# A two-layer diffusion trunk on one Trainium2 core: normed loads put first in the sync queue, and one context product moved into the group before

## The chip, the cores and the metric

The kernel runs on one core of one Trainium2 chip. Its time is the device time of one execution in microseconds (us), given as the median of several runs; lower is better.

## The reference

Two layers work on 1024 latent tokens and 256 context tokens of width 1024. Layer 0 mixes the tokens by attention and a linear recurrence side by side, layer 1 by neighbourhood attention; each layer then has a feed-forward part (ConvFFN). The change lies where layer 0 goes from its mixer to its ConvFFN, in these lines:

```python
y_lat = jnp.concatenate([oa_lat, readout(ob_lat, bg_l)], axis=-1) @ w_out
x = x + g1 * rms_norm(y_lat, norm_post_mix[l])
h_lat = rms_norm(x, norm_pre_ffn[l]) * (1.0 + sc2) + sh2
x = x + g2 * rms_norm(conv_ffn(h_lat, ...), norm_post_ffn[l])
# the same for the context tokens, with their own modulation

def conv_ffn(h, w_up, conv_w, conv_b, w_down):
    u = h @ w_up                                   # 1024 -> 5632
    u = depthwise_width_3_conv(u) + conv_b         # over the positions
    a, g = jnp.split(u, 2, axis=-1)
    return (jax.nn.silu(g) * a) @ w_down
```

## The kernel before

**Arithmetic.** Every fp32 operand of a product is split into a high and a low part (names that end in h and l), and each product is three matmuls: high by high, high by low, low by high. All matmuls come from one helper, so nearly all have line L120; they are told apart by tile names.

**The end of the mixer** (`even_attention`). Five blocks of 256 tokens (the context first, then four of latent tokens) go through attention; `project` is a generator that multiplies finished blocks by the output weights (tiles `g_ps`) in small steps, given out between the attention's own steps by `step(n)`. Each output tile of 128 tokens has closing work, kept in the list `late` and taken from it one piece at a step: root mean square, gate, residual, the store of the new stream to `x1d`, a second root mean square, a scaling on ScalarE (L1038), and the store of the normed tile to the DRAM tensor `xnd` (L1039). There are ten such tiles: 8 and 9 are the context, 0 to 7 the latent tokens. Tile 7 is closed last. `step` does nothing while the next block is not ready.

**The start of the ConvFFN** (`ffn_up`, and in it `up_front`, for layer 0). The ten tiles are loaded back from `xnd` as `n_x` (L1413), 512 KB each. TensorE transposes them (L1147) into three PSUM banks in turn (`n_pv`, `n_pc`, `n_pt`); ScalarE applies scale and shift (L1148); VectorE and ScalarE split the results. First come the context tiles (8, 9), then the first half of the latent tokens (tiles 0 to 3), then the second half (4 to 7), then sums of these.

**The up projection** is done by 22 groups. A group takes 128 columns of each of the two halves of `w_up`, two loads of 512 KB named `w_raw` (L1333), and forms the latent product by a scheme of seven block products in place of eight: A11·B11, A12·B21, S2·T2, S1·T1, S3·T3, A22·T4 and S4·B22, where A and S are weights and their sums, and B and T are activations and their sums. They go into the banks `u_g` and `u_v`. The context product has two halves of 24 matmuls of 256 columns each, one with A11 and A12 and one with A21 and A22, into the bank `u_pc`. In group 0 the sums T1, T3, T4 and the split of B22 are still being made, between the products that read them.

**What sets the order.** Inside `in_order(engines)` the instructions of those engines keep the order in which the code is written. `even_attention` does this for all engines and the sync queue (SyncE, SP in the profile); `ffn_up` for the four computing engines only, so that its DMAs on the sync queue are ordered by a scheduler. A DMA waits in its queue for its semaphores, and those behind it in the queue wait with it. Memory is handed from a closed pool to the next when the last reader of the overlapped tiles is done. The loop over the groups, at the start of a group:

```python
                if ctx and j:
                    pc = pp.tile([P, 512], F32, name="u_pc", bufs=1)
                    product(pc[:, :256], ("A11", "A12"), "ctx", True, True)
                elif ctx:
                    pc = st["pc"]
```

Here `j` is the group, and `st["pc"]` is the tile that `up_front` filled for group 0.

Of the kernel before, what the change touches and what calls it, by code (L numbers as in the profile page):

```python
# [11 lines left out]
F32 = mybir.dt.float32  # L12
# [8 lines left out]
P = 128  # L21
D = 1024
# [43 lines left out]
class Trunk:  # L66
# [785 lines left out]
    def even_attention(self, gp, tp, pp, sp):  # L852
# [5 lines left out]
        nc, a = self.nc, self.a  # L858
# [3 lines left out]
        st = {}  # L862
# [8 lines left out]
        def load_gate(kind):  # L871
            g = st["gate"] = sp.tile([P, D], F32, name="gate", bufs=1)
            nc.sync.dma_start(g, self.gated[0, 0, kind].partition_broadcast(P))
# [117 lines left out]
        def gated(b, k):  # L991

            step(32 * b - at[0])
            split(b, BH + k, st["g", b][:, k, :])
            if k == BH - 1:
                st["ready"] = b

        def squares(y, ms):
            junk = sp.tile([P, 512], BF16, name="yjunk", bufs=1)
            for h in range(2):  # L1000
                nc.scalar.activation(junk, y[:, 512 * h:512 * h + 512], AF.Square, scale=1.0 / 32.0, accum_out=ms[:, h:h + 1])

        def project():

            late = []
            for b, (n0, kind) in enumerate(blocks):
                for i in range(2):
                    y = sp.tile([P, D], F32, name="y", bufs=2)
                    ms = self.small.tile([P, 2], F32, name="y_ms")
                    for half in range(2):  # L1010
                        ps = gp.tile([P, 512], F32, name="g_ps")
                        for k in range(KT):
                            xhk, xlk = (o[:, i * P:(i + 1) * P] for o in st["o", b, k])
                            whk, wlk = (w[:, 512 * (k % 2):512 * (k % 2) + 512] for w in W[4 * half + k // 2])
                            self.mm(ps, xhk, whk, k == 0, False)
                            self.mm(ps, xhk, wlk, False, False)
                            self.mm(ps, xlk, whk, False, k == KT - 1)
                            if late:
                                late.pop(0)()
                            yield b  # L1020
                        late.append(lambda ps=ps, y=y, ms=ms, half=half: self.y_half(ps, y, ms, half, sp))
                        if half == 0:
                            xt = sp.tile([P, D], F32, name="y_x", bufs=2)
                            r = n0 + i * P
                            nc.sync.dma_start(xt, a["ctx"][i * P:(i + 1) * P] if kind else a["x"][r:r + P])
                        else:
                            late.append(lambda ms=ms: st.update(r=self.y_rstd(ms)))
                            late.append(lambda: None)
                            late.append(lambda: None)
                            late.append(lambda y=y: self.y_norm(y, st["r"], st["gate"]))  # L1030
                            late.append(lambda y=y, xt=xt: nc.vector.tensor_tensor(out=y, in0=y, in1=xt, op=OP.add))
                            late.append(lambda: None)
                            late.append(lambda y=y, r=r: nc.gpsimd.dma_start(self.x1d[r:r + P], y))
                            ms2 = self.small.tile([P, 2], F32, name="y_ms")
                            late.append(lambda y=y, ms2=ms2: squares(y, ms2))
                            late.append(lambda ms2=ms2: st.update(r2=self.y_rstd(ms2)))
                            late.append(lambda: None)
                            late.append(lambda y=y, xt=xt: nc.scalar.mul(xt, y, st["r2"]))  # L1038
                            late.append(lambda xt=xt, r=r: nc.gpsimd.dma_start(self.xnd[r:r + P], xt))  # L1039
                    if b == 0 and i == 1:  # L1040
                        late.append(lambda: load_gate(0))
            while late:
                late.pop(0)()

        fill, todo, at = project(), [], [0]

        def step(n):

            for _ in range(n):
                if at[0] < 32 * (st.get("ready", -1) + 1):  # L1050
                    next(fill, None)
                    at[0] += 1

        zeros = sp.tile([P, 2 * LINE], F32, name="zeros", bufs=1)[:, 0:1]
        nc.gpsimd.memset(zeros, 0.0)
# [2 lines left out]
        with self.in_order(*self.compute, E.SP):  # L1058
# [9 lines left out]
            for s in range(N + 8):  # L1068
# [11 lines left out]
                t = transposes(pair - 2, half) if 0 <= pair - 2 < len(pairs) else iter(())  # L1080
# [243 lines left out]
    def ffn_up(self, l, src, ctx, x_src, x_dst, hp, pp, tp, es, beside):  # L1324


        nc, a = self.nc, self.a
        raws, W, S, st = {}, {}, {}, {}

        def load(j, s):  # L1330
            if j < FK:
                raws[j, s] = self.wp.tile([P, 1024], F32, name="w_raw", bufs=3)
                nc.sync.dma_start(raws[j, s], a["w_up"][l, j + FK * s])  # L1333
# [19 lines left out]
        def product(ps, ws, x, start, stop):  # L1353

            jobs = [(W[w], k) for w in ws for k in range(4)]
            for i, ((wh, wl), k) in enumerate(jobs):
                h, lo = wh[:, k * P:(k + 1) * P], wl[:, k * P:(k + 1) * P]
                xhk, xlk = X[x][i]
                self.mm(ps, h, xhk, start and i == 0, False)
                self.mm(ps, h, xlk, False, False)  # L1360
                self.mm(ps, lo, xhk, False, stop and i == len(jobs) - 1)

        def add(out, x, y):
            nc.vector.tensor_tensor(out=out, in0=x, in1=y, op=OP.add)  # L1364
# [36 lines left out]
        def up_front():  # L1401
# [3 lines left out]
            xs, turn = {}, [0]  # L1405
            tags = dict(zip((8, 9, 0, 1, 2, 3, 4, 5, 6, 7), ["x_T" + x for x in ("20h", "20l", "21h", "21l", "30h", "30l")] +
                            ["x_T1" + x for x in ("0h", "0l", "1h", "1l")]))
            for i, t in tags.items():
                if i == 4:
                    load(0, 0)  # L1410
                    load(0, 1)
                xs[i] = hp.tile([P, D], F32, name="n_x", tag=t, bufs=1)
                nc.sync.dma_start(xs[i], self.xnd[i * P:(i + 1) * P])  # L1413

            def places():
                turn[0] += 1
# [103 lines left out]
        with self.in_order(*self.compute, behind=l == 1), ExitStack() as loads:  # L1520
# [3 lines left out]
            for j in range(FK):  # L1524
                n = j + 1
                if n == FK:
                    loads.enter_context(self.in_order(mybir.EngineType.SP))
                    down = self.ffn_down(l, ctx, x_src, x_dst, hp, sp, pp, tp, beside)
                    next(down)
                if ctx and j:  # L1530
                    pc = pp.tile([P, 512], F32, name="u_pc", bufs=1)
                    product(pc[:, :256], ("A11", "A12"), "ctx", True, True)
                elif ctx:
                    pc = st["pc"]
# [26 lines left out]
                        split(n, "A12")  # L1561
                Z = st["G", j][:, 512:]
                product(Z, ("S1",), "T1", True, False)
                u2 = st["u2"] = half("f_u2")
                add(u2, V[:, 512:], st["p1"])
                if j == 0:
# [1061 lines left out]
```

## Time and profile before

| | us |
|---|---|
| median of 3 runs | 3382.82 |
| the three runs | 3382.82, 3382.61, 3395.19 |
| the profiled execution | 3393.66 |
| its span, first to last instruction | 3391.9 |
| TensorE busy in it | 3124.3 (92%) |
| last matmul of layer 0's mixer starts at | 1109.08 |
| first transpose of layer 0's ConvFFN starts at | 1123.67 |
| group 1 of the up projection starts at | 1195.20 |

Times inside the execution count from the start of the span. PE is TensorE, PEld its weight loads, DVE VectorE, ACT ScalarE, POOL GpSimd, and SPq the DMA issues of the sync queue. A row of the timeline holds start, duration, engine, line, operation, out<-in with shapes, and in brackets how long the engine had been idle before it and what ended that.

### The profile page before, as it was taken

The numbers are of one execution on the slowest core, as the hardware profiler recorded it, in microseconds if no ns is written. First come the engines' busy times: TensorE is split into PE (matmuls) and PEld (weight loads), VectorE is DVE, ScalarE is ACT, GpSimd is POOL, SyncE is SP. The second block draws the span as 40 slices with busy tenths as digits, with TensorE's granted clock in tenths as the row PEclk, the third lists the DMA queues.
The fourth block names the chain that finished last, engine by engine and source line by source line (L and its number), as shares of the span: only waits on it lengthen the run. The fifth ranks groups of instructions, "written<-read, shape, count | busy, mean of one in ns | idle before, by whom it ended". The sixth has DMA issues, their size and how long they took to land.

```text
span 3391.9 us, 48795 instructions
## 1 busy us (share of the span) xinstructions
PE 3124.3 (92%) x18364; PEld 2569.4 (76%) x18364; DVE 2020.3 (60%) x3405; ACT 1501.8 (44%) x2681; POOL 1545.7 (46%) x1173
## 2 busy tenths in 40 slices
PE   5999998869999699999999979999998989999997
PEld 2777776658887488888878758889886758888785
DVE  3635666647776654454567873367775465555777
ACT  3322222256665543343434353366665543434443
POOL 1310110187775466666620011477775367777201
PEclk8999999979999799999999989999998979999998
DMA  6534333321111321111275783222224212222855
GB/s 235 156 98 138 119 130 108 114 89 44 63 57 68 121 73 69 65 70 69 74 258 180 276 247 128 79 60 71 63 59 158 102 62 81 87 81 81 279 183 208
DMA packets 202540, 398.73 MB, mean 118 GB/s; under 512 B 23344, under 2 KB 84784, under 8 KB 202304
## 3 DMA queue, kind: packets, MB, share of 16 engines
q1 hardware_dynamic: 191680, 358.38, 31.7%
q0 software_dynamic: 10624, 37.23, 2.9%
q8 instruction: 144, 2.36, 0.3%
q14 instruction: 92, 0.75, 0.1%
HBM read 316.86 MB, written 79.06 MB: 117 GB/s over the span
## 4 chain that ended last, share of the span: by engine, by line
PE 75%; DVE 10%; ACT 4%; DMA 4%; issue 3%; POOL 2%; SPq 1%; ACTq 0%; POOLq 0%; DVEq 0%
PE g_ps L120 21%; PE u_g L120 13%; PE u_v L120 10%; PE d_ps L120 10%; PE u_pc L120 4%; PE a_pv L120 2%; PE c_pv L120 2%; PE c_s L120 2%; PE a_pt L950 2%; PE c_pt L2258 2%; PE mod_ps L120 1%; DVE a_pl L952 1%; PE a_s L120 1%; PE o_ps L120 1%; ACT a_ph L951 1%
## 5 line engine op out<-in xcount | busy, mean ns | idle before, releaser
L128 POOL TENSOR_TENSOR rs_r<-rs_e,mhalf 128x1 f32<-128x1 f32 (+3 forms) x106 | 80.7, 761 | 953.0 <-DVE rs_e L127 952.9
L120 PE MATMUL d_ps<-d_Bh,d_Ah 128*128 128x512 f32 x704 | 278.0, 395 | 12.0 <-ACT d_Bh L1672 11.9
L120 PE MATMUL d_ps<-d_Bl,d_Ah 128*128 128x512 f32 x704 | 278.4, 396 | 3.4 <-DVE d_Bl L1673 2.7
L120 PE MATMUL d_ps<-d_Bh,d_Al 128*128 128x512 f32 x704 | 277.3, 394 | 2.0 <-DVE d_Al L1673 1.9
L2241 POOL TENSOR_SCALAR c_p<-c_p,rl 128x640 f32<-128x640 f32 (+1 forms) x128 | 232.2, 1815 | 96.3 <-DVE rl L2240 58.9
L930 POOL TENSOR_SCALAR a_p<-a_p,rl 128x1280 f32<-128x1280 f32 (+1 forms) x80 | 240.2, 3007 | 56.8 <-DVE rl L929 52.5
L120 PE MATMUL g_ps<-xh,w_hi 128*128 128x512 f32 (+1 forms) x640 | 259.6, 406 | 6.3 <-ACT w_hi L564 4.9
L120 PE MATMUL g_ps<-xh,w_lo 128*128 128x512 f32 (+1 forms) x640 | 240.3, 376 | 2.5 <-POOL w_lo L2141 1.3
L120 PE MATMUL g_ps<-xl,w_hi 128*128 128x512 f32 (+1 forms) x640 | 240.8, 376 | 0.0
L952 DVE TENSOR_TENSOR a_pl<-a_pt,a_ph 128x512 fp32r<-128x512 f32 (+1 forms) x200 | 119.0, 603 | 92.3 <-ACT a_ph L951 92.3
L1364 DVE TENSOR_TENSOR f_u<-u_v,f_p 128x512 f32<-128x512 f32 x88 | 60.5, 688 | 188.5 <-PE u_v L120 188.5
L120 PEld LDWEIGHTS d_ps<-d_Bh,d_Ah 128*128 128x128 f32 x704 | 133.9, 190 | 42.0 <-ACT d_Bh L1672 13.5
L1350 POOL TENSOR_TENSOR w_S4l<-w_s,w_S4h 128x512 fp32r<-128x512 f32 x44 | 57.0, 1297 | 233.8 <-ACT w_S4h L1349 233.8
L120 PEld LDWEIGHTS d_ps<-d_Bl,d_Ah 128*128 128x128 f32 x704 | 133.9, 190 | 36.2 <-DVE d_Bl L1673 7.7
L120 PEld LDWEIGHTS g_ps<-xh,w_hi 128*128 128x128 f32 x640 | 123.9, 194 | 45.8 <-issue 27.7
L120 PEld LDWEIGHTS d_ps<-d_Bh,d_Al 128*128 128x128 f32 x704 | 133.8, 190 | 30.9 <-DVE d_Al L1673 3.3
L951 ACT CAST a_ph<-a_pt 128x512 fp32r<-128x512 f32 (+1 forms) x200 | 101.9, 518 | 108.7 <-PE a_pt L950 108.6
L2261 DVE TENSOR_TENSOR c_pl<-c_pt,c_ph 128x256 fp32r<-128x256 f32 (+1 forms) x256 | 113.1, 470 | 58.5 <-ACT c_ph L2260 57.3
L120 PE MATMUL g_ps<-w_hi,xh 128*128 128x512 f32 (+1 forms) x368 | 142.7, 388 | 3.1 <-DVE xh L2015 2.1
L120 PEld LDWEIGHTS g_ps<-xh,w_lo 128*128 128x128 f32 x640 | 123.4, 193 | 25.8 <-POOL w_lo L2141 1.7
L120 PE MATMUL g_ps<-w_lo,xh 128*128 128x512 f32 (+1 forms) x368 | 138.5, 376 | 3.7 <-DVE w_lo L2002 2.9
L120 PE MATMUL g_ps<-w_hi,xl 128*128 128x512 f32 (+1 forms) x368 | 138.6, 377 | 0.2 <-DVE xl L300 0.2
(543 smaller groups left out, 9873.5 us busy)
## 6 DMA issues: line engine op xcount, KB each, us to landing
m_raw<-in_w_mod SPq DMA_DIRECT2D x96, 512.0 KB
w_raw<-in_w_up SPq DMA_DIRECT2D x88, 512.0 KB
d_rawA<-actd SPq DMA_DIRECT2D x77, 512.0 KB
d_rawB<-in_w_down SPq DMA_DIRECT2D x74, 512.0 KB
actd<-f_t SPq DMA_DIRECT2D x22, 640.0 KB
d_t<-in_w_down SPq DMA_DIRECT2D x22, 512.0 KB
actd<-f_t SPq DMA_DIRECT2D x22, 512.0 KB
d_s<-actd SPq DMA_DIRECT2D x20, 512.0 KB
```

Source lines behind the costliest of these rows:

```text
L120: return self.nc.tensor.matmul(out, lhsT, rhs, start=start, stop=stop, skip_group_check=True, **k)
L128: nc.gpsimd.tensor_tensor(out=r[:p, :n], in0=e[:p, :n], in1=self.mhalf[:p, :n], op=OP.pow)
L930: nc.gpsimd.tensor_scalar(Pt[:, :nk], Pt[:, :nk], rl, None, op0=OP.mult)
L950: nc.tensor.transpose(pt[:, m, qt * P:(qt + 1) * P], Pt[:, kts[j + m] * P:(kts[j + m] + 1) * P], self.ident)
L951: nc.scalar.copy(ph[:, j:j + n], pt[:, :n])
L952: nc.vector.tensor_tensor(out=pl[:, j:j + n], in0=pt[:, :n], in1=ph[:, j:j + n].bitcast(F32), op=OP.subtract)
L1350: nc.gpsimd.tensor_tensor(out=lo, in0=part(j, name), in1=hi.bitcast(F32), op=OP.subtract)
L1364: nc.vector.tensor_tensor(out=out, in0=x, in1=y, op=OP.add)
L2241: nc.gpsimd.tensor_scalar(Pt[:, :n], Pt[:, :n], rl, None, op0=OP.mult)
L2258: nc.tensor.transpose(pt[:, j, :], Pt[:, (src + j) * P:(src + j + 1) * P], self.ident)
L2261: nc.vector.tensor_tensor(out=vap(pl, o, dims), in0=pt[:, :cnt], in1=vap(ph, o, dims).bitcast(F32), op=OP.subtract)
```

## The change

Three edits, all in layer 0.

1. The list `late` is made outside `project`, and `step` takes a piece from it when the next block is not ready. In the built program the order on ScalarE, VectorE and GpSimd is row by row what it was: at no step that finds its block not ready does the list hold anything.
2. The loop that loads the ten `n_x` tiles keeps its written order on the sync queue.
3. The first half of group 1's context product (24 matmuls) is written in group 0, behind S1·T1 and ahead of S3·T3, into the transposes' bank `n_pt`. Groups 2 to 21 are as they were.

```diff
+        late = []
+
         def project():
-            late = []
             for b, (n0, kind) in enumerate(blocks):
...
                 if at[0] < 32 * (st.get("ready", -1) + 1):
                     next(fill, None)
                     at[0] += 1
+                elif late:
+                    late.pop(0)()
...
-            for i, t in tags.items():
-                if i == 4:
-                    load(0, 0)
-                    load(0, 1)
-                xs[i] = hp.tile([P, D], F32, name="n_x", tag=t, bufs=1)
-                nc.sync.dma_start(xs[i], self.xnd[i * P:(i + 1) * P])
+            with self.in_order(mybir.EngineType.SP):
+                for i, t in tags.items():
+                    if i == 4:
+                        load(0, 0)
+                        load(0, 1)
+                    xs[i] = hp.tile([P, D], F32, name="n_x", tag=t, bufs=1)
+                    nc.sync.dma_start(xs[i], self.xnd[i * P:(i + 1) * P])
...
-                if ctx and j:
+                if ctx and j > 1:
                     pc = pp.tile([P, 512], F32, name="u_pc", bufs=1)
                     product(pc[:, :256], ("A11", "A12"), "ctx", True, True)
                 elif ctx:
                     pc = st["pc"]
...
                 Z = st["G", j][:, 512:]
                 product(Z, ("S1",), "T1", True, False)
+                if ctx and j == 0:
+                    st["pc"] = tp.tile([P, 512], F32, name="u_pc", tag="n_pt", bufs=1)
+                    product(st["pc"][:, :256], ("A11", "A12"), "ctx", True, True)
```

The sync queue, between the last load of the mixer and the third weight load. The numbers tell the tiles apart: `n_x_11128` and `11130` are tiles 8 and 9, `11132` to `11138` tiles 0 to 3, `11144` to `11150` tiles 4 to 7; `w_raw_11140` and `11142` are the weights of group 0, `11233` the first of group 1. Before:

```order
L1025 DMA y_x_11035<-in_x 128x1024
L1333 DMA w_raw_11140<-in_w_up 128x1024
L1333 DMA w_raw_11142<-in_w_up 128x1024
L1413 DMA n_x_11144<-xnd_80 128x1024
L1413 DMA n_x_11146<-xnd_80 128x1024
L1413 DMA n_x_11148<-xnd_80 128x1024
L1333 DMA w_raw_11233<-in_w_up 128x1024
L1413 DMA n_x_11128<-xnd_80 128x1024
L1413 DMA n_x_11130<-xnd_80 128x1024
L1413 DMA n_x_11132<-xnd_80 128x1024
```

The same place in the change:

```order
L1026 DMA y_x_11035<-in_x 128x1024
L1417 DMA n_x_11128<-xnd_80 128x1024
L1417 DMA n_x_11130<-xnd_80 128x1024
L1417 DMA n_x_11132<-xnd_80 128x1024
L1417 DMA n_x_11134<-xnd_80 128x1024
L1417 DMA n_x_11136<-xnd_80 128x1024
L1417 DMA n_x_11138<-xnd_80 128x1024
L1336 DMA w_raw_11140<-in_w_up 128x1024
L1336 DMA w_raw_11142<-in_w_up 128x1024
L1417 DMA n_x_11144<-xnd_80 128x1024
L1417 DMA n_x_11146<-xnd_80 128x1024
```

The context tiles and tiles 0 to 3 have moved ahead of the weights and of tiles 4 to 6; the third weight load now comes behind tile 7 and behind the load of the convolution's taps (`cw`).

TensorE in group 0, between S1·T1 (`x_T11` with `w_S1`) and S3·T3 (`x_T30` with `w_S3`). Before:

```order
L120 MATMUL u_g<-x_T11h,w_S1h 128x512
L120 MATMUL u_g<-x_T11l,w_S1h 128x512
L120 MATMUL u_g<-x_T11h,w_S1l 128x512
L120 MATMUL u_v<-x_T30h,w_S3h 128x512
L120 MATMUL u_v<-x_T30l,w_S3h 128x512
L120 MATMUL u_v<-x_T30h,w_S3l 128x512
```

In the change, the last rows of the product that has come between:

```order
L120 MATMUL u_pc<-x_ctx3h,w_A12h 128x256
L120 MATMUL u_pc<-x_ctx3l,w_A12h 128x256
L120 MATMUL u_pc<-x_ctx3h,w_A12l 128x256
L120 MATMUL u_v<-x_T30h,w_S3h 128x512
L120 MATMUL u_v<-x_T30l,w_S3h 128x512
L120 MATMUL u_v<-x_T30h,w_S3l 128x512
```

The 24 matmuls of `u_pc` stand in front of S3·T3. TensorE from group 0 to group 1, between S4·B22 (`x_B221` with `w_S4`) and what follows, before:

```order
L120 MATMUL u_g<-x_B221h,w_S4h 128x512
L120 MATMUL u_g<-x_B221l,w_S4h 128x512
L120 MATMUL u_g<-x_B221h,w_S4l 128x512
L120 MATMUL u_pc<-x_ctx0h,w_A11h 128x256
L120 MATMUL u_pc<-x_ctx0l,w_A11h 128x256
```

And in the change:

```order
L120 MATMUL u_g<-x_B221h,w_S4h 128x512
L120 MATMUL u_g<-x_B221l,w_S4h 128x512
L120 MATMUL u_g<-x_B221h,w_S4l 128x512
L120 MATMUL u_g<-x_B210h,w_A12h 128x512
L120 MATMUL u_g<-x_B210l,w_A12h 128x512
```

Group 1 now opens with A12·B21 (`x_B210` with `w_A12`); the context product is gone from there.

## The prediction

> **What bounds the kernel now.** I read the page first (engines, chain), then the PE's waits, then a table by stage around the change, then the timeline of each engine there.
>
> ```profile
> PE 3124.3 (92%) x18364; PEld 2569.4 (76%) x18364; DVE 2020.3 (60%) x3405; ACT 1501.8 (44%) x2681; POOL 1545.7 (46%) x1173
> PE n_pv L1147 <- DMA n_x<-xnd: 15.7, 2, 14.2
> 1109.50:1123.70 14.20, 0.03 (x1) 0.06 (x1) 3.73 (x7) 3.28 (x7) 2.24 (x4) 0.62 0.96 354
> 1123.70:1155.50 31.80, 25.99 (x140) 19.86 (x140) 22.55 (x36) 22.44 (x38) 12.37 (x9) 0.85 0.25 102
> 1165.90:1195.20 29.30, 17.34 (x36) 10.05 (x37) 20.22 (x28) 12.79 (x22) 14.10 (x11) 0.65 0.17 54
> 1195.20:1740.00 544.80, 542.06 (x2858) 467.58 (x2856) 276.74 (x308) 215.00 (x299) 343.87 (x247) 1.00 0.24 85
> ```
>
> A stage row is length, then busy time of PE, PEld, DVE, ACT and POOL, clock, DMA share, GB/s. TensorE bounds the whole, and from 1195.2 the up projection runs on it without a gap (542.06 of 544.80): what arrives there earlier ends earlier. Ahead of that it stands still twice: 14.2 us for `n_x`, the longest wait of its kind in the trace, with the DMA engines full (0.96), and some 12 us in group 0 (29.30 less 17.34), where VectorE has the larger share.
>
> **The closing pieces** (edit 1) move nothing, since the built order on ScalarE, VectorE and POOL is the old one: 0.
>
> **The loads** (edit 2). The sync queue before:
>
> ```profile
> 1099.94 0.33 SPq L1025 DMA_DIRECT2D y_x<-in_x  x1
> 1109.50 1.00 SPq L1333 DMA_DIRECT2D w_raw<-in_w_up  x2
> 1110.55 1.39 SPq L1413 DMA_DIRECT2D n_x<-xnd  x3
> 1111.98 0.47 SPq L1333 DMA_DIRECT2D w_raw<-in_w_up  x1
> 1112.55 13.85 SPq L1413 DMA_DIRECT2D n_x<-xnd  x7
> 1134.07 0.33 SPq L1464 DMA_DIRECT2D cw<-in_convT  x1
> 1082.41 1.19 PE a_pv L120 x10
> ```
>
> After the last `y_x` the queue stands until the last matmul of the mixer frees the weights' memory (1109.5); then two weights, tiles 4 to 6 and one more weight go ahead of the context tiles that TensorE needs first. In the change, tiles 8, 9 and 0 to 3 stand behind `y_x`, and what they wait for on the way (scores and values of the attention's last heads; the last row, from the chain of waits) is over by 1083.6. They issue from 1100.3, six at about 0.4 us each. The slowest rate seen here: eight loads from 1109.50 until tile 9 lets its transpose start at 1125.65 are 4.2 MB in 16.2 us, 260 GB/s. At that rate `y_x` and the context tiles (1.57 MB) are in by 1106.4, and all seven (3.7 MB) by 1114.4.
>
> The end of the wait is then no longer a load:
>
> ```profile
> 1117.21 1.15 ACT L1038 ACTIVATE y_x<-y,rs_r 128x1024 f32<-128x1024 f32 x1 [1.12 <-POOL rs_r L128]
> 1126.16 0.56 ACT L1148 ACTIVATE n_t<-n_pv,mod,mod 128x256 f32<-128x256 f32 x1 [7.80 <-PE n_pv L1147]
> 1147.44 0.62 ACT L1349 CAST w_A11h<-w_raw 128x512 fp32r<-128x512 f32 x1 [0.34 <-issue]
> 1125.65 0.47 PE L1147 MATMUL n_pv<-ident,n_x 128*128 128x128 f32 x1 [1.53 <-DMA n_x<-xnd]
> 1139.50 0.60 PE L1147 MATMUL n_pc<-ident,n_x 128*128 128x128 f32 x4
> 1118.65 0.57 POOL L1039 DMA_DIRECT2D xnd<-y_x  x1 [1.48 <-ACT y_x L1038]
> xnd<-y_x POOLq DMA_DIRECT2D x4, 512.0 KB, 3.0
> ```
>
> TensorE can fill its three transpose banks at about 1111, but ScalarE, whose order is kept, first closes tile 7; its scaling ends at 1118.36. So of the 14.2 us only ScalarE's own gap goes, **7.8 us**. From 1126.16 to group 0 the work is a chain of ScalarE and VectorE with TensorE between, none of it tied to the clock on the wall, and it moves by 7.8 as a whole, if the other loads keep up.
>
> Each queue neighbour has room. Tile 7 is read back after its store, issued at 1118.65. Before, that store had full DMA engines beside it and the last `n_x` issued only at 1126.4 (end of the row of seven). Even then, with the 3.0 us from issue to landing that the last row has for 512 KB, tile 7 is there at 1129.4, and is wanted at 1139.50 − 7.8 = 1131.7. Behind it wait `cw` and the first weight of group 1, which by the same 3.0 us lands at about 1130 and is wanted at 1147.44 − 7.8 = 1139.6. Group 0's weights issue at 1109.5 as before. So 0 for these; if tile 7 were later than 1131.7 each us would cost one.
>
> **The context product** (edit 3). The new place, TensorE and then VectorE:
>
> ```profile
> 1165.47 0.40 PE L120 MATMUL u_g<-x_T11h,w_S1l 128*128 128x512 f32 x1
> 1167.48 0.49 PE L120 MATMUL u_v<-x_T30h,w_S3h 128*128 128x512 f32 x1 [1.61 <-ACT x_T30h L1133]
> 1168.82 0.50 PE L120 MATMUL u_v<-x_T30l,w_S3h 128*128 128x512 f32 x1 [0.85 <-DVE x_T30l L1136]
> 1171.15 0.79 PE L120 MATMUL u_v<-x_T30h,w_S3h 128*128 128x512 f32 x1 [1.60 <-ACT x_T30h L1133]
> 1167.45 1.31 DVE L1136 TENSOR_TENSOR x_T30l<-x_t,x_T30h 128x512 fp32r<-128x512 f32 x1 [0.68 <-ACT x_T30h L1133]
> ```
>
> The chain of waits gives the prices of the products:
>
> ```profile
> 1144.44 0.74 PE u_g L120 x2
> 1146.05 2.88 PE u_pc L120 x24
> 1149.80 2.75 PE u_g L120 x12
> 1183.91 4.73 PE u_v L120 x11
> 1190.99 4.37 PE u_g L120 x11
> ```
>
> The product takes 2.88 us. Put in at 1165.70 it ends at 1168.58, and the second matmul of S3·T3 could not start before 1168.76 anyway; 1.6 us more of slack follow. So it costs nothing where it goes and takes 2.88 us from the full stretch after 1195.2. Part of this comes back in group 1, where the rest isn't faster:
>
> ```profile
> 1210.42 0.56 ACT L1367 ACTIVATE f_t<-u_pc,cw 128x256 f32<-128x256 f32 x1 [0.66 <-DMA actd<-f_t]
> 1213.17 0.48 DVE L1372 SCALAR_TENSOR_TENSOR f_t<-u_pc,cw,f_t 128x255 f32<-128x255 f32 x1
> 1214.80 0.69 DVE L1364 TENSOR_TENSOR f_u<-u_v,f_p 128x512 f32<-128x512 f32 x1 [1.15 <-PE u_v L120]
> 1215.53 0.70 DVE L1364 TENSOR_TENSOR u_v<-u_g,f_u 128x512 f32<-128x512 f32 x1
> 1214.61 0.39 PE L120 MATMUL u_g<-x_B110h,w_A11h 128*128 128x512 f32 x1
> ```
>
> The convolution of group 1's context waits for the store of group 0's result (0.66 us on the DMA), which hangs on group 0's VectorE work, not on the product. VectorE is free at 1213.65 in both kernels; it then makes `f_u` and the sum that reads `u_g` (0.73 and 0.70 us), 1215.08, and S4·B22 may not write `u_g` before that. TensorE, which starts the twelve matmuls ahead of it at 1214.61 (last row) and ends them 2.75 later (the chain's row for twelve), would be there at 1217.36 − 2.88 = 1214.48. So 0.6 us are lost, and **2.3 us** stay. At worst the gain is 0 (VectorE as late as 1217.4), at best 2.88; I take 2.3, being read from the rows.
>
> **The clock.**
>
> ```profile
> 1112.00:1116.00 4.00, 0.00 (x0) 0.00 (x0) 2.49 (x2) 1.35 (x4) 0.56 (x1) 0.62 1.01 373
> 1132.00:1136.00 4.00, 3.33 (x21) 2.83 (x20) 3.90 (x7) 3.94 (x7) 1.51 (x2) 0.82 0.08 23
> 1168.00:1172.00 4.00, 1.53 (x3) 0.58 (x3) 3.32 (x3) 0.62 (x1) 3.50 (x3) 0.88 0.27 108
> 1184.00:1188.00 4.00, 4.00 (x10) 3.13 (x11) 1.67 (x3) 3.03 (x6) 2.97 (x2) 0.50 0.01 2
> 1182.76 0.80 PE L120 MATMUL u_v<-x_T40h,w_A22h 128*128 128x512 f32 x1 [5.39 <-ACT x_T40h L1133]
> ```
>
> The granted clock (third number from a row's end) falls to half after the long wait (0.62 in the row of 1112: 0.96 us full and 3.04 half, so at about 1113.0), is back by the same reckoning at about 1133.4, and falls again at about 1171.0, so that A22·T4 and most of S4·B22 ran at half (4.73 and 4.37 us for eleven). The Trainium skill (TensorE: Matmul & The Clock Gate, "What's actually happening") says that the clock is judged by free-running windows of 3.413 us, halved after an idle one and restored after a busy one; the trace agrees, the three edges lying 20.4 and 37.6 us apart, 6 and 11 such windows. In the change TensorE still idles from about 1112 to 1118 and still 5.4 us before A22·T4, so I add 0, with ±2 us for where the edges fall.
>
> **The sum.** 7.8 + 2.3 = 10.1 us. The profiled execution took 3393.66 (span 3391.9), so it would take 3383.6. It lies 10.8 above the median of 3382.82, close to the slowest run shown (3395.19); I carry the difference over: **3372.7 us**. That is 0.3%, less than the 0.5% (16.9 us) that a measurement of this kernel can tell from no change.
>
> **The rivals.**
> *The clock stays full.* The moved product keeps TensorE busy through a gap, the fall at 1171.0 is avoided, and A22·T4 and S4·B22 run at full rate. Eleven matmuls at 2.75/12 are 2.5 us: 2.2 + 1.9 = 4.1 more, 3368.6. Against it: the 5.39 us of idle, which the product doesn't touch. Chance 0.10. By the window rule just named the fall merely comes later.
> *The loads alone.* The 2.3 us come back too, in group 1 or behind it: 3375.0, chance 0.09.
> *A new wait for the same stage.* The 3.1 MB issued at 1100.3 hold up what closes tile 7 or brings it back, and ScalarE starts the context no sooner: 3380.5. It decides if `y_x` lands later than 1113.3, or tile 7 later than 1139.5. Against it, `y_x` is ahead in the same queue. Chance 0.06.
> *Slower: half clock through the front.* TensorE now works in short bursts from 1111, is judged idle longer, and the five products of twelve and two of 24 up to 1165.9 all run at half: 5 × 2.75 + 2 × 2.88 = 19.5 more, 3392.2, and more if it lasts into group 1. It decides if the clock isn't back by 1136.6 (1144.4 − 7.8, where products begin to set the time). Against it, the transposes brought it back at 1133.4. Chance 0.05.
> *The level of the run.* The runs shown lie 12.6 us apart, and one trace doesn't say why: with the forecast's gain the upper level gives 3385.3 (0.09), and if the cause of the upper level lies in this wait too, the other way, 3360.1 (0.11).
>
> **The numbers.** The forecast has the remaining 0.50, with 3369 to 3377 as its own range. From 3365 to 3386 lie the forecast, the first three rivals and the upper level, 0.84 less their tails, so 8 in 10. Faster by over 0.5% (below 3365.9): 0.11 and 0.03 from the clock rival's best end, 0.14. Slower by over 0.5% (above 3399.7): 0.03, from the slow rival where it lasts. Within: 0.83.
>
> **What would show it.** The first `n_x` issues at about 1100.3, the wait for `n_x` is gone from the PE's list, and the first `n_t` follows directly on the last L1038, 7.8 us earlier. `u_pc` of group 1 lies before S3·T3 with no later start of the second matmul there; group 1's S4·B22 shows a wait of some 0.6 us for VectorE; the start of group 2 is 10 us earlier. I am wrong if a wait for `n_x` is left, if tile 7 is waited for, or if the clock is half between 1137 and 1158.

## The result, and the profile after

| | before | changed |
|---|---|---|
| median of 7 runs each, us | 3385.20 | 3373.03 |
| lowest and highest | 3382.61, 3395.19 | 3368.97, 3377.46 |
| changed to before, with 95% interval | | 0.9956 [0.9940, 0.9971] |
| profiled execution; its span | 3393.66; 3391.9 | 3373.03; 3371.3 |

The changed kernel is 12.2 us (0.36%) faster in the medians. Its time lies within the forecast's own range, its gain below the 0.5% (16.9 us) named there, and the interval of the ratio does not hold 1. First, the waits of the PE in the changed kernel (engine, line waited for, us in total, times, longest). Line numbers are 1 to 4 higher than before.

```profile
PE n_pv L1150 <- ACT n_t L1151: 7.0, 1, 7.0
```

The row for `n_x`, 14.2 us in one piece before, is gone from the whole list. In its place TensorE, its three banks filled, waits 7.0 us for ScalarE to empty the first. The reason is in the timelines of the sync queue and of ScalarE, changed kernel:

```profile
1096.49 0.33 SPq L1026 DMA_DIRECT2D y_x<-in_x  x1
1096.91 2.88 SPq L1417 DMA_DIRECT2D n_x<-xnd  x6
1106.05 0.96 SPq L1336 DMA_DIRECT2D w_raw<-in_w_up  x2
1107.06 13.26 SPq L1417 DMA_DIRECT2D n_x<-xnd  x4
...
1113.77 1.15 ACT L1039 ACTIVATE y_x<-y,rs_r 128x1024 f32<-128x1024 f32 x1 [1.12 <-POOL rs_r L128]
1114.82 0.55 ACT L1151 ACTIVATE n_t<-n_pv,mod,mod 128x256 f32<-128x256 f32 x1
```

Six `n_x` issue 0.42 us after `y_x`, where the first `n_x` stood 10.6 us behind it before, and the first `n_t` follows tile 7's scaling without a gap (before, 7.80 us lay between). The table by stage (length, then busy time of PE, PEld, DVE, ACT and POOL, granted clock, DMA share, GB/s) has the end of the mixer in its first row, then group 0 up to S1·T1, the rest of group 0, and the groups up to layer 0's down projection:

```profile
1105.63:1115.42 9.79, 1.26 (x8) 0.64 (x7) 3.76 (x8) 3.79 (x9) 1.88 (x4) 0.70 1.02 413
1115.42:1155.94 40.52, 35.44 (x182) 28.03 (x183) 32.17 (x46) 26.98 (x45) 19.66 (x14) 0.86 0.23 81
1155.94:1185.22 29.28, 18.71 (x61) 12.12 (x60) 20.47 (x28) 12.79 (x22) 14.37 (x11) 0.71 0.17 54
1185.22:1740.00 554.78, 551.75 (x2889) 475.07 (x2889) 287.45 (x319) 220.84 (x306) 344.09 (x247) 1.00 0.26 92
```

The DMA engines are still full in the first row (1.02), but no engine waits for them there. The third row holds the moved product: 61 matmuls, where the stretch before had 36 in a nearly equal 29.30 us.

By the starts that the timelines show, the two profiles and the spread over all thirteen profiles of this case (us):

| stretch | before | changed | all thirteen |
|---|---|---|---|
| start to the first matmul of attention's scores | 726.5 | 723.0 | 719.4 to 728.6 |
| on to the mixer's last matmul | 382.6 | 382.6 | 379.4 to 384.1 |
| on to the first `n_t` (**first stage**) | 17.08 | 9.19 | by kernel |
| on to group 2 (**second stage**) | 93.89 | 92.41 | by kernel |
| on to the first matmul of the down projection | 495.9 | 495.9 | 495.9 to 496.0 |
| on to the end | 1675.9 | 1668.1 | 1668.1 to 1677.9 |

Of the 20.6 us between the two spans only 7.9 + 1.5 lie where the code changed. The rest lies in stretches whose code is the same, and which differ by up to 10 us between any two profiles. So the two stages are read from the profiles, and whole times are compared only over repeated runs.

### The profile page after: what moved, and what is told of

Its sections match the earlier page's. It is cut to its first block, busy times and chain, and to the rows that moved or that the text cites. A ratio compares the mean times of both kernels' runs of the same rounds, so it can differ in the third digit from the quotient of the medians.

```text
span 3371.3 us, 48796 instructions
## 1 busy us (share of the span) xinstructions
PE 3117.5 (92%) x18364; PEld 2566.5 (76%) x18364; DVE 2020.2 (60%) x3405; ACT 1502.2 (45%) x2681; POOL 1548.6 (46%) x1173
## 4 chain that ended last, share of the span: by engine, by line
PE 77%; DVE 10%; ACT 4%; issue 3%; DMA 3%; POOL 2%; SPq 0%; POOLq 0%; ACTq 0%; DVEq 0%
PE g_ps L120 21%; PE u_g L120 14%; PE d_ps L120 11%; PE u_v L120 10%; PE u_pc L120 4%; PE a_pv L120 2%; PE c_pv L120 2%; PE c_s L120 2%; PE a_pt L950 2%; PE c_pt L2265 2%; PE mod_ps L120 1%; DVE a_pl L952 1%; PE a_s L120 1%; PE o_ps L120 1%; ACT a_ph L951 1%
## 5 line engine op out<-in xcount | busy, mean ns | idle before, releaser
L930 POOL TENSOR_SCALAR a_p<-a_p,rl 128x1280 f32<-128x1280 f32 (+1 forms) x80 | 240.2, 3005 | 56.7 <-DVE rl L929 52.3
L2267 ACT CAST c_ph<-c_pt 128x256 fp32r<-128x256 f32 (+1 forms) x256 | 98.4, 414 | 91.0 <-PE c_pt L2265 88.9
```

What stands on the lines that cost most here:

```text
L930: nc.gpsimd.tensor_scalar(Pt[:, :nk], Pt[:, :nk], rl, None, op0=OP.mult)
L2267: nc.scalar.copy(vap(ph, o, dims), pt[:, :cnt])
```

## The experiments

The theory: 7.9 us come from the place of the loads in the sync queue, up to the point where tile 7's closing on ScalarE takes over; the product adds some 2 us in the second stage; edit 1 adds nothing. The rivals: one part alone, the early start rather than the place in the queue, or the clock. All ratios are to the kernel before, measured beside it.

| | us, median (runs) | before, us | ratio [95%] | first stage | second stage |
|---|---|---|---|---|---|
| e1, without edit 3 | 3377.44 (12) | 3385.23 | 0.9977 [0.9967, 0.9987] | 9.19 | 95.32, dip |
| e2, edit 3 alone | 3383.06 (12) | 3385.23 | 0.9996 [0.9985, 1.0006] | 16.83 | 90.39 |
| e3, edit 1 alone | 3386.74 (11) | 3385.23 | 1.0006 [0.9997, 1.0015] | 16.43 | 94.05 |
| e4, weights first | 3377.99 (12) | 3385.23 | 0.9979 [0.9969, 0.9988] | 10.97 | 91.44 |
| e5, closing by halves | 3375.91 (5) | 3387.47 | 0.9961 [0.9949, 0.9974] | 8.33 | 91.14 |
| e6, gaps filled | 3374.49 (6) | 3387.47 | 0.9958 [0.9945, 0.9970] | 9.18 | 92.42, dip |
| e7, and early copy | 3377.42 (9) | 3387.47 | 0.9970 [0.9958, 0.9981] | 9.19 | 90.03 |
| e9, the change again | 3376.05 (8) | 3387.47 | 0.9963 [0.9950, 0.9976] | 9.19 | 90.48 |
| e10, halves and early copy | 3372.64 (5) | 3385.91 | 0.9956 [0.9943, 0.9969] | 8.32 | 92.46, dip |
| e8, all of these | 3372.70 (5) | 3385.91 | 0.9954 [0.9942, 0.9966] | 8.32 | 90.82 |
| e11, the change a third time | 3375.89 (5) | 3385.91 | 0.9965 [0.9952, 0.9979] | 9.18 | 92.35, dip |

"Dip" marks profiles with 3.4 us of half clock in the middle of the front, the stretch from the first `n_t` to group 0's products; the section on the prediction tells of it. The first profile of the change has it too (92.41); the one of before has not.

**e1, the loads without the product.**

```diff
-                if ctx and j > 1:
+                if ctx and j:
...
-                if ctx and j == 0:
-                    st["pc"] = tp.tile([P, 512], F32, name="u_pc", tag="n_pt", bufs=1)
-                    product(st["pc"][:, :256], ("A11", "A12"), "ctx", True, True)
```

> The change without its third edit: the loads in order, the context product of group 1 back at group 1's start. My theory (the wait for the loads gives way to ScalarE's closing of tile 7, and the product adds its own part): from the start of the mixer's last matmul to the first n_t 9.2 us, as in the changed kernel (before 17.1); from there to the start of group 2's context product about 94 us, as before; 7.8 us faster than before. Rival (the product is worth nothing beside the loads): the same time as the full change, and the second stage about 92.6.

The first stage is 9.19 us, as in the change, and the time falls by 7.8 us (3377.44 against 3385.23; 4.4 to 11.2 by the interval). The loads carry most of the gain. The second stage, expected at about 94, is 95.32, with the dip.

**e2, the product alone**, put into the kernel before.

```diff
-                if ctx and j:
+                if ctx and j > 1:
...
+                if ctx and j == 0:
+                    st["pc"] = tp.tile([P, 512], F32, name="u_pc", tag="n_pt", bufs=1)
+                    product(st["pc"][:, :256], ("A11", "A12"), "ctx", True, True)
```

> The kernel before with the third edit alone. My theory: first stage 17.1 us as before, from the first n_t to group 2's context product 91.2 (all of the 2.88 us) to 92.6 (what the changed kernel's profile shows); 1.5 to 2.9 us faster than before. Rival (the product comes back in group 1 or behind it): second stage 94, no difference in time. Rival (the edits only work together): also no difference.

The second stage is 3.5 us shorter in the profile (90.39 against 93.89; expected were 91.2 to 92.6). The time falls by 1.4 by the ratio (0.9996; by the medians 2.2), and the interval reaches from 5.1 faster to 2.0 slower: the runs alone can't show the sign. TensorE's timeline in this kernel has a wait that I had not named, at the first matmul of group 1, and ScalarE's timeline its cause:

```profile
1195.60 0.50 PE L120 MATMUL u_g<-x_B210h,w_A12h 128*128 128x512 f32 x1 [1.30 <-ACT f_p L1386]
1193.87 1.20 ACT L1367 ACTIVATE f_t<-u_v,cw 128x1024 f32<-128x1024 f32 x1 [4.34 <-DVE u_v L1364]
1194.97 0.58 ACT L1386 COPY f_p<-u_g 128x512 f32<-128x512 f32 x1
```

A12·B21 writes to the bank that ScalarE has first to copy to `f_p`, and the copy stands behind the start of a convolution that waits for VectorE. The context product used to run in these 1.3 us.

**e3, the closing pieces alone.**

```diff
+        late = []
 ...
-            late = []
 ...
+                elif late:
+                    late.pop(0)()
```

> The kernel before with the first edit alone. My theory: the built program is the one of before, so ratio 1 within the interval, both stages as before (17.1 and 94.0 us), and its runs spread as those of before, which also shows how far two profiles of one program lie apart ahead of the change's place and behind it. Rival (the handing out of closing pieces does something): a first stage that is shorter.

Ratio 1.0006 with an interval that holds 1, stages like those of before: edit 1 moves nothing. The three profiles with the old order of the loads (before, e2 and e3) have 17.08, 16.83 and 16.43 us in the first stage, so against the 9.19 of the change the loads gain 7.2 to 7.9 us there, and 7.89 is the upper end.

**e4, the change with group 0's weights ahead of the `n_x` loads.**

```diff
-                    if i == 4:
+                    if i == 8:
                         load(0, 0)
                         load(0, 1)
```

> The change with group 0's two weight loads written ahead of the ten normed loads, so that the sync queue stands until the mixer's last matmul, as before, but the context tiles come fourth and fifth in it (before: seventh and eighth). It tells the early start from the place in the queue. By the rate of before, 2.0 us a load, tile 9 is there some 10 us after the last matmul: first stage about 11 us (before 17.1, changed 9.2), and the whole about 2 us slower than the change. Rival (only the early start counts): first stage near 17, about 8 us slower than the change. Rival (the place in the queue is all): first stage 9.2, same as the change.

Here the queue stands until the mixer's last matmul (at 1101.67) frees the weights' memory; then the context tiles go directly behind the weights. The sync queue's timeline and the PE's wait list of this kernel:

```profile
1102.09 1.51 SPq L1336 DMA_DIRECT2D w_raw<-in_w_up  x3
1103.70 15.26 SPq L1417 DMA_DIRECT2D n_x<-xnd  x10
...
PE n_pv L1150 <- DMA n_x<-xnd: 9.6, 2, 8.6
...
PE n_pt L1150 <- DMA n_x<-xnd: 1.6, 2, 0.8
```

The wait for `n_x` is back, and yet the first stage is only 1.8 us longer than in the change (10.97). So 6.1 of the first stage's 7.9 us (5.5 to 6.1 by the three old profiles) come from tiles 4 to 6 no longer being ahead of the context tiles; loading before the mixer's end brings the last 1.8. It brings some 1.1 more in the second stage: there the transposes into `n_pt` wait for `n_x` too (1.6 us, the last row), and S1·T1 starts 37.81 us after the first `n_t`, where it is 36.7 in every other profile without the dip.

**e5, tile 7's closing by halves**: VectorE's gate and residual and ScalarE's square run on 512 columns at a time, and half of the scaling goes to VectorE.

```diff
+        def by_halves(y, xt, ms2):
+            for h in range(2):
+                c = slice(512 * h, 512 * h + 512)
+                nc.vector.scalar_tensor_tensor(out=y[:, c], in0=y[:, c], scalar=st["r"], in1=st["gate"][:, c], ...)
+                nc.vector.tensor_tensor(out=y[:, c], in0=y[:, c], in1=xt[:, c], op=OP.add)
+                nc.scalar.activation(junk, y[:, c], AF.Square, scale=1.0 / 32.0, accum_out=ms2[:, h:h + 1])
...
+            nc.scalar.mul(xt[:, :512], y[:, :512], st["r2"])
+            nc.vector.tensor_scalar(xt[:, 512:], y[:, 512:], st["r2"], None, op0=OP.mult)
```

> The change, with the closing work of tile 7 done in two halves of 512 columns (gate, residual and squares by halves, the scaling half on ScalarE and half on VectorE). Theory (with the loads early, the closing of tile 7 on ScalarE is what the context waits for): some 0.7 us go because the first half's squares run beside VectorE's second half, some 0.5 because ScalarE scales half a tile; first stage 9.2 to 7.9 us, the whole about 1.3 us faster than the change. Rival (the normed loads or the memory of the mixer's banks end the wait): first stage stays at 9.2.

ScalarE's timeline in it:

```profile
1113.19 0.63 ACT L1011 ACTIVATE yjunk<-y 128x512 bf16<-128x512 f32 x1 [3.30 <-DVE y L1009]
...
1116.41 0.72 ACT L1014 ACTIVATE y_x<-y,rs_r 128x512 f32<-128x512 f32 x1 [1.12 <-POOL rs_r L128]
1117.04 0.55 ACT L1171 ACTIVATE n_t<-n_pv,mod,mod 128x256 f32<-128x256 f32 x1
```

The first `n_t` is again directly behind the scaling, and the stage is 0.86 us shorter (8.33). I had expected 7.9. What the context waits for is thus tile 7's closing, as the prediction has it. Over the whole time 0.9 us can't be seen: 0.9961 beside 0.9963 for the change (e9).

**e6 and e7, the clock.** e6 adds 36 matmuls to group 0's gaps whose results are overwritten; e7 also puts the copy to `f_p` ahead of the convolution's start.

```diff
+                def keep(i):
+                    for _ in range((5, 5, 4, 22)[i]):
+                        self.mm(V[:, :512], W["A22"][0][:, :P], X["T2"][0][0], True, True)
-                product(V[:, 512:], ("S3",), "T3", False, True)
+                product(V[:, 512:], ("S3",), "T3", False, True, keep if ctx and j == 0 else None)
```

> The change with 36 matmuls more, whose results are thrown away: 5, 5 and 4 behind the first three thirds of group 0's S3.T3 and 22 behind its last, into the bank that A22.T4 then overwrites, so that TensorE does not stand still there. Theory (the gaps of group 0 halve the clock and A22.T4, S4.B22 pay for it): clock 1.00 up to S4.B22, A22.T4 2.7 instead of 4.5 to 5.1 us, group 2 starts 1.5 to 2.5 us earlier after the first n_t than in the change (92.4), and A12.B21 of group 1 waits for ScalarE's copy f_p. Rival (VectorE's chain sets the end of group 0 whatever the clock): no difference. Rival (the matmuls more delay S3.T3 and A22.T4): up to 2 us slower.

> As the kernel with 36 matmuls more, and ScalarE's copy f_p of group 0 ahead of its convolution start instead of behind it. The product-only kernel showed TensorE waiting 1.3 us for this copy before A12.B21 of group 1, a wait that the forecast had not seen. Theory: that wait goes, and the start of group 2 comes up to 1.3 us earlier than with the 36 matmuls alone. Rival (the bank u_v or VectorE's f_u is next at once): the wait moves to S2.T2 or S3.T3 of group 1 and nothing is gained; the copy ahead of the convolution start may even cost 0.5 us on ScalarE.

Neither gains: 0.9958 and 0.9970 beside 0.9963. Compared at the same state of the dip, e6's second stage is the change's own (92.42 to 92.41 and 92.35), and e7's 90.03 is 0.45 less than e9's 90.48. In e6 the clock still fell during A22·T4. In e7 it did not: after its first matmul the product's other eleven took 2.8 us, where the chain of waits of the changed kernel has 4.45. TensorE's timeline of e7 shows where the gain went:

```profile
1179.29 0.47 PE L120 MATMUL u_g<-x_B220h,w_S4h 128*128 128x512 f32 x1 [1.61 <-DVE u_v L1369]
1180.85 0.50 PE L120 MATMUL u_g<-x_B220l,w_S4h 128*128 128x512 f32 x1 [1.09 <-DVE x_B220l L1139]
```

S4·B22 waits 1.09 us for VectorE's `x_B220l`, a wait that is 0.3 us in e9. So with A22·T4 at full clock VectorE decides when S4·B22 can go on, and most of S4·B22 still ran at half here; where it ran at full, in e2 and e4, TensorE then waited for the copy. No run has both products at full clock.

**e9, the change again**, beside e5 to e7.

> The changed kernel once more, for more runs beside the others on one chip and a second profile of it. Theory: ratio to before 0.9970 to 0.9978 (7.8 us of the loads and 1.5 to 2.9 of the product, 9.3 to 10.7 us), less than the 0.9956 of the first seven runs; first stage 9.2; the stage up to group 2 anywhere between 90.4 and 92.6, by where the clock falls to half. Rival (0.9956 holds: the edits bring more together than apart): 0.9956 again.

The first stage is 9.19 again, the second 90.48, without the dip. The ratio, 0.9963, lies between the 0.9970 of the theory and the rival's 0.9956, and its interval holds 0.9956 as well as 0.9970.

**e10, e8 and e11**: e5 with the early copy alone, e5 with all of e7, and the change a third time, together.

```diff
+                if ctx and j == 0:
+                    first_out(n)
                 add(V[:, :512], V[:, :512], u3)
...
-                else:
+                elif not (ctx and j == 0):
                     first_out(n)
```

> The changed kernel with tile 7's last closing work done by halves (half of its final scaling on VectorE) and, in group 0, ScalarE's copy f_p written ahead of the convolution's start instead of behind it; nothing is added to TensorE. My theory: the two are on the path one behind the other. The first stage (last mixer matmul to first n_t) goes from 9.2 to 8.3 us, as with the halves alone, and group 1's A12-B21 waits no longer for f_p (1.3 us), which shortens the stretch from the first n_t to group 2 by at most that, to about 89.1 where the changed kernel has 90.5 with its clock edges well placed. Together 2.2 us less than the changed kernel, about 0.9954 of the kernel before where the change has 0.9961. Rival: what A12-B21 no longer waits for it waits for one place later, at S4-B22 of group 0 for x_B220l (1.1 us in the run with throw-away matmuls and the early copy); then the stretch stays at 90 to 92.4 and only the 0.9 of the halves is left, 0.9958.

> The same as the run before with the 36 throw-away matmuls in group 0's gaps added (their results are overwritten). My theory: the clock stays full up to A22-T4, but VectorE's chain of sums sets group 0's length, so nothing is gained over the run without them: the stretch from the first n_t to group 2 is 89 to 91 us, and the ratio lies within 0.0005 of that run. Rival: the clock sets it, A22-T4 and S4-B22 take 2.8 us for eleven matmuls in place of 4.4, the stretch goes to 86 to 87 and the ratio falls by 0.001.

> The changed kernel itself a third time, as the measure for the two runs beside it. My theory: 0.9956 to 0.9963 of the kernel before, first stage 9.2 us, stretch from the first n_t to group 2 between 90.5 and 92.4 by where the clock's edges fall. Rival: if the gain hung on the level of a run and not on the change, the ratio would lie outside 0.995 to 0.997 in this third set.

Both kernels with halves have the first stage at 8.32. e10's second stage, expected at about 89.1, is 92.46 with the dip, beside 92.35 in e11: the early copy brings nothing there. The rival's reason for this is not tested by e10, since in its profile, as in the change's, S4·B22 ran mostly at half clock and TensorE did not wait for the copy anyway; it is in e7 that the wait for `x_B220l` is seen. e11's ratio, 0.9965, is just outside the 0.9956 to 0.9963 expected and within its rival's bounds of 0.995 to 0.997. With the gaps filled, TensorE's timeline and the chain of waits of e8 show why full gaps don't pay:

```profile
1169.22 0.49 PE L120 MATMUL u_v<-x_T40h,w_A22h 128*128 128x512 f32 x1 [0.93 <-ACT x_T40h L1156]
1170.38 0.68 PE L120 MATMUL u_v<-x_T40l,w_A22h 128*128 128x512 f32 x1 [0.66 <-DVE x_T40l L1159]
...
1166.44 2.80 DVE x_t L1210 x4
1170.38 4.39 PE u_v L120 x11
```

The wait ahead of A22·T4 is 0.93 us and not 5.39, but its start hangs on VectorE's sums all the same (56.7 us after the first `n_t`, in e9 56.6), and the clock fell anyway: the window of the table by stage that holds both remaining waits was 1.81 us busy, the next ran at half, and eleven matmuls took 4.39 us.

```profile
1167.13:1170.54 3.41, 1.81 (x8) 0.97 (x7) 3.41 (x6) 1.92 (x4) 0.24 (x1) 1.00 0.00 0
1170.54:1173.95 3.41, 3.41 (x9) 2.65 (x10) 1.59 (x3) 2.96 (x6) 2.46 (x2) 0.50 0.01 2
```

The two kernels lie 3.2 us under the change beside them (3372.64 and 3372.70 to 3375.89), with intervals that overlap almost wholly. The first stage accounts for 0.9 of it, and that the rest is more than chance isn't shown.

## Why the prediction was right, and where it was off

**The closing pieces: 0**, and e3 says 0.

**The loads: 7.8 forecast, 7.2 to 7.9 in the first stage, 7.8 in the time of e1.** The chain was the forecast one: early place in the queue, banks filled, ScalarE's closing of tile 7 last. e4 splits the term by its two causes, e5 shows what it ends on. No load of the change is waited for behind it: neither tile 7 nor a weight appears among the PE's waits.

**The product: 2.3 forecast, 2.9 in the second stage.** The second stages by state:

| | without the product | with it at the new place |
|---|---|---|
| no dip | 93.89, 94.05 | 90.39, 90.48, 91.14, 91.44 |
| dip | 95.32 | 92.35, 92.41, 92.42, 92.46 |

(e7 and e8 are left out; e6 and e10 stand in the last cell with their extra edits, since they show nothing of them.) With the dip the difference is 2.9; without it, from 2.5 to 3.7, because the clock over A22·T4 and S4·B22 and, in e4, the late loads lie in it too. The starts of the products, which the timelines give, separate the parts (us):

| stretch | before | changed | e1 | e2 | e9 |
|---|---|---|---|---|---|
| first `n_t` to S1·T1 | 36.68 | 38.28 (dip) | 38.24 (dip) | 36.69 | 36.66 |
| on to A22·T4 | 19.92 | 19.94 | 19.91 | 19.95 | 19.98 |
| on to S4·B22 | 7.48 | 7.20 | 7.37 | 6.78 | 6.86 |
| on to group 1's A12·B21 | 7.84 | 4.97 | 7.85 | 4.88 | 4.89 |
| on to group 2 | 21.97 | 22.01 | 21.96 | 22.10 | 22.09 |

The fourth row, from which the product was taken out, falls from 7.8 to 4.9 us; the second, into which it was put, and the last, group 1, are what they were to within 0.15 us.

At the new place it costs nothing, as forecast. TensorE's timeline of the changed kernel:

```profile
1155.72 0.39 PE L120 MATMUL u_g<-x_T11h,w_S1l 128*128 128x512 f32 x1
...
1158.82 0.39 PE L120 MATMUL u_v<-x_T30h,w_S3h 128*128 128x512 f32 x1
1159.11 0.50 PE L120 MATMUL u_v<-x_T30l,w_S3h 128*128 128x512 f32 x1
...
1161.44 0.49 PE L120 MATMUL u_v<-x_T30h,w_S3h 128*128 128x512 f32 x1 [1.61 <-ACT x_T30h L1136]
...
1173.05 0.79 PE L120 MATMUL u_v<-x_T40h,w_A22h 128*128 128x512 f32 x1 [5.39 <-ACT x_T40h L1136]
```

From S1·T1's last matmul to A22·T4 it is 17.33 us; before it was 17.29 (1165.47 to 1182.76). Both waits that were expected to stay are there, 1.61 and 5.39.

The term that was wrong is the 0.6 us to be lost in group 1. The forecast held VectorE free at the same moment in both kernels, since the convolution of the context waited for the store of group 0's result. ScalarE's timeline of before, which I had not read one row further up, and that of the changed kernel with VectorE's next row:

```profile
1209.14 0.62 ACT L1349 CAST w_S1h<-w_s 128x512 fp32r<-128x512 f32 x1 [1.37 <-PE u_g L120]
...
1197.71 0.61 ACT L1352 CAST w_S1h<-w_s 128x512 fp32r<-128x512 f32 x1
1198.60 0.57 ACT L1370 ACTIVATE f_t<-u_pc,cw 128x256 f32<-128x256 f32 x1 [0.27 <-DMA actd<-f_t]
1202.00 0.69 DVE L1367 TENSOR_TENSOR f_u<-u_v,f_p 128x512 f32<-128x512 f32 x1 [0.16 <-PE u_v L120]
```

Before, two things ended at nearly the same time ahead of `f_t`: the cast of `w_S1h`, which had stood 1.37 us for TensorE's S1·T1 and ended at 1209.76, and the store, whose last packet ended at 1209.83. The cast came forward with TensorE. The store, whose issue follows VectorE, became shorter, as the DMA's rates show, before (40 slices from 1203 to 1212) and changed (from 1193 to 1200):

```profile
GB/s 0 0 0 0 0 0 0 0 0 0 0 0 0 0 159 482 410 364 364 341 432 273 0 0 23 23 46 23 23 23 0 0 0 0 0 0 0 0 0 0
GB/s 0 0 0 94 0 0 0 0 0 0 0 0 0 0 0 0 0 0 0 439 439 410 410 380 439 351 410 468 0 0 0 0 0 0 0 0 0 0 0 0
```

Before, the store's last seven packets end singly, 0.19 us apart (the 23s and the 46). One 16 KB packet of the queue that the profile calls `q8 instruction` ran from 1206.43 to 1207.90, within the store. In the changed kernel that packet (the 94) is over at 1194.78, before the store begins, and the store needs 2.6 us from its issue to its last packet. It is 2.6 in all ten profiles with the moved product, and 3.9 to 4.3 in the three without it, each time with the instruction packet inside it. The packet starts 8.1 to 8.7 us after group 1's A12·B21, and in e6 to e8, which have 36 matmuls more, none comes from 5 to 12 us after it. So its time follows TensorE's work, and with the product it moved out of the store's way. That it holds up part of the store is inferred from these times, not shown by a run of its own. At 4.3 us the changed kernel's store would have ended at 1199.9, 1.3 us after `f_t` started (an estimate), and time would have been lost after all.

After A12·B21's start, `f_t` is at 12.34 us before (1210.42 − 1198.08) and at 13.38 now (1198.60 − 1185.22): 1.04 later and not 2.88. The slack that `f_u` had, 1.15 us of waiting for TensorE, takes this up; 0.16 of it is left. So nothing is lost there, and group 1 from A12·B21 to group 2 is 22.0 us in both kernels (1220.05 − 1198.08, 1207.23 − 1185.22).

What it overlooked in turn is the copy to `f_p`, shown at e2. It costs 1.3 us in e2 and 1.4 in e4, where S4·B22 ran at full clock, and nothing in the change's three profiles, where TensorE reached A12·B21 later than the copy.

**The clock: 0 ± 2.** The chain of waits of the changed kernel has the two products that were expected to stay at half clock, A22·T4 and S4·B22 (its row goes on into A12·B21), and, new, group 0's own context product, which is slower than it was:

```profile
1135.81 3.36 PE u_pc L120 x24
1174.20 4.45 PE u_v L120 x11
1181.01 7.14 PE u_g L120 x23
```

The 3.36 was 2.88 before. Rows of the stage table, cut at the clock's edges, show the dip: two of the changed kernel, then the window over the same work in e9 and in e2, by the edges of each:

```profile
1129.99:1133.40 3.41, 1.65 (x6) 0.78 (x5) 3.41 (x3) 0.77 (x2) 2.44 (x2) 1.00 0.00 0
1133.40:1136.81 3.41, 3.41 (x16) 3.13 (x15) 1.10 (x3) 1.55 (x2) 0.00 (x0) 0.50 0.00 0
...
1134.51:1137.92 3.41, 2.35 (x14) 1.75 (x14) 2.57 (x3) 0.19 (x1) 1.42 (x1) 1.00 0.00 0
1143.35:1146.76 3.41, 2.14 (x11) 1.52 (x12) 2.78 (x3) 0.00 (x0) 1.61 (x1) 1.00 0.00 0
```

TensorE does the same work in each kernel here. Where a window of 3.41 us happens to hold its thinnest stretch, 1.65 us busy, the next one runs at half. Where the windows cut it otherwise (2.35, 2.14) the clock stays. Three profiles of the one changed kernel have it, have it not, and have it (92.41, 90.48, 92.35). Up to S1·T1 it costs 1.6 us (38.28 and 36.66 in the table above), inside the ± 2, and is why the first profile's second stage shows a gain of 1.5 only. It ended at 1136.81, just ahead of the 1137 from which half clock was to show the forecast wrong. The Trainium skill (TensorE: Matmul & The Clock Gate, "What's actually happening") has the clock halved after an idle window; the trace differs: a window that was busy for 1.65 of 3.41 us, its longest pause about 1 us, was enough. The same was so before the change: the window ahead of the fall at 1171.0 was busy for 1.10 us (last section). So the trace bears the prediction out on the length of the windows, and not on what makes one idle.

**The sum.** 7.9 and 2.9 make 10.8; forecast were 10.1. Measured are 12.2, 11.4 and 10.0 in the medians of the three sets of the change, each against the kernel before beside it. The forecast time came out within 0.4 us partly by luck: it was taken from a median of three runs of before, 3382.82, and over more runs before lies at 3385.2 to 3387.5. Of the rivals, the loads alone (3375.0) is against e1's and the change's second stages (95.32 to 92.41), not against the runs: e2's interval holds it. The new wait and the slower front did not come: the first stage is as short as forecast, and after 1123.2 the front has no half clock beyond the dip. That the clock stays full, by 4.1 us, is not borne out: A22·T4 was at half in the change, and in e8 even with the gap ahead of it filled; in e7, where it was at full, the second stage was only 0.45 us shorter. The two levels of the run (3385.3, 3360.1) lie outside the seven runs of the change.

What stays open: why e2, 3.5 us shorter in its second stage, shows 1.4 in its time; its interval holds both.

## What to carry to other kernels

Before a DMA queue is reordered, look for what is next in line behind the wait it removes: here a closing chain on ScalarE made 7.8 us out of 14.2, and the place behind other loads was worth more than the early start. When work is moved out of a gap's cover, list all that had been finishing under it (here a copy that frees a bank), and before a wait is taken as fixed, read the row ahead of it on its engine and see what shares the DMA engines with its named releaser. For gains below what run-to-run spread allows, compare the stretch that was touched over several profiles, cut at the starts of its products, and only those whose clock edges fall alike.

## What was not expected of the hardware

In the dip a window with TensorE busy for 1.65 of 3.41 us was followed by half clock, and so was one of 1.81 us in e8; at the dip's place windows of 1.85 us (e3) and more kept the clock. But the busy time that the profile shows does not decide it. Two pairs of neighbouring windows, cut at the clock's edges, the first pair before, the second in e5:

```profile
1164.18:1167.60 3.42, 1.81 (x8) 1.00 (x7) 2.74 (x4) 1.17 (x2) 2.69 (x3) 1.00 0.29 93
1167.60:1171.01 3.41, 1.10 (x3) 0.36 (x3) 2.85 (x2) 0.53 (x1) 3.33 (x3) 1.00 0.41 149
...
1162.03:1165.44 3.41, 2.09 (x6) 0.97 (x6) 2.69 (x4) 0.62 (x2) 0.48 (x1) 1.00 0.00 0
1165.44:1168.85 3.41, 2.53 (x5) 0.79 (x3) 1.37 (x3) 2.64 (x5) 1.97 (x2) 0.50 0.00 0
```

Before, 1.81 us busy kept the full clock for the next window, and 1.10 us lost it at 1171.01; in e5, 2.09 us lost it. The return is no clearer. In the changed kernel the transposes alone brought the clock back:

```profile
1116.34:1119.75 3.41, 2.97 (x12) 1.59 (x10) 3.13 (x10) 2.97 (x6) 0.19 (x1) 0.50 0.85 345
1119.75:1123.16 3.41, 3.41 (x17) 3.05 (x16) 3.12 (x6) 3.38 (x7) 2.40 (x2) 0.50 0.45 154
```

Behind the first, 2.97 us busy, the clock stayed at half for another window; behind the second, busy throughout, it was full. Earlier in the same trace a window of 2.72 us (689.66 to 693.07) brought it back. What is counted in a window stays open. The same program, run again, cuts its work by these windows elsewhere, and 1.6 us of this kernel hang on that in the front and some 0.3 us (7.20 and 6.86) from A22·T4 to S4·B22.
